# Where the state-space mixer's phase doublings and weight sums stand in the first gate-and-up stage

## The chip, the cores and the metric

The kernel runs on one core of one Trainium2 chip. The metric is the device time of one execution in microseconds (us). Three runs of the kernel before gave 2377.18, 2378.55 and 2381.32 us.

The engines are named as in the profile: PE is TensorE (matrix products, PEld its weight loads), DVE is VectorE, ACT is ScalarE, POOL is GpSimd, and SP is the engine whose queue issues all the DMA transfers spoken of here. Every engine works through its own instructions in a fixed order, and waits on semaphores for the others.

## The reference: what is computed

Two layers on a sequence of 1024 tokens of width 1024, in float32. Layer 0 mixes tokens by attention with a forget gate, layer 1 by a state-space mixer called S5. Behind each mixer comes a dense SwiGLU:

```
def swiglu(h, w_gate, w_up, w_down):
    return (jax.nn.silu(h @ w_gate) * (h @ w_up)) @ w_down
```

The S5 mixer needs, for 64 groups of 64 states, powers of a complex number `a` and a scaled input matrix:

```
    mag = jnp.exp(lam_re * dt)
    a_re = mag * jnp.cos(lam_im * dt)
    a_im = mag * jnp.sin(lam_im * dt)
...
    bb_re = z_re[..., None] * b_re - z_im[..., None] * b_im
    bb_im = z_re[..., None] * b_im + z_im[..., None] * b_re
```

None of these parameters depends on the tokens. So the kernel works them out long before layer 1 begins, beside the gate and up products of layer 0. The change lies there.

## The kernel before

**Gate and up.** `gate_up` runs once in each layer. It multiplies the normalized tokens by `w_gate` (called m = 0) and `w_up` (m = 1). It does so with a scheme that needs seven block products in place of eight, so sums and differences of the weight blocks are formed first. The 22 column blocks of each matrix are taken in 11 pairs, p = 0 to 10 (blocks p and p + 11). A pair has 14 steps on PE, two (m = 0, 1) for each of the seven products in `steps`; steps 0 and 1 are A11, 2 and 3 A12, 4 and 5 S1, 6 and 7 S2, 8 and 9 S3, 10 and 11 S4, 12 and 13 A22. A step is 4 blocks of k times 3 matmuls: each operand is split in a high part (`ah`, rounded by ACT, line 851) and a low part (`al`, the rest, by DVE, line 852), and three of the four products of parts are taken. All these matmuls are on line 882.

**Banks.** A step's result goes to a bank of PSUM: X for steps 0, 1, 6 to 9, 12 and 13, Y for steps 2 and 3, Z for steps 4, 5, 10 and 11, one bank for each m. X has two sets that alternate between pairs. Each step is evicted before its bank can be written again: steps 0 and 1 by an ACT copy (line 932), 2 and 3 by a DVE addition (line 934), 4 to 7 by ACT copies (lines 937 and 939), 8 and 9 by DVE (line 941), 10 and 11 by DVE (line 944). ACT applies silu on line 920.

**Weights of the next pair.** `load` fetches raw weight pages, on SP, as pages come free. `sa` forms the sums S1 and S2 (lines 864 and 865), `sb` S3 and S4 (lines 870 and 871) in the raw page itself. `prep` says behind which step each is written down; the scheduler may queue them sooner.

**The mixer's parameters.** `s5_params`, with `s5_small` in it, is a generator. It is carried on by a bit at the steps listed in the table `first`, which stands in `trunk` (pairs 0, 1 and 2; 5 and 12 in the others). Among its pieces are:
- the powers of `a` (`powers`, with `cmul`, lines 1211 to 1216);
- the phases `ph` of 15 multiples of an angle, by doubling: n = 1, 2, 4, 8, six DVE operations each (lines 1184 to 1189), on tiles of 64, 128, 256 and 448 elements a partition;
- `bb`, a `cmul` of 128x512 with the raw `b` (tile s5w0) and scratch (tile s5w1), and on ACT copies of it to `bs` (line 1272);
- the loads of `c_re` and `c_im` (line 1233) onto the pages of those two tiles, and their transposes on PE (line 1239), which ACT copies out to `cc` (line 1243);
- tables for 8 chunks of groups, built on POOL (lines 1269 to 1332).

The phases are read by `s5_rot`, which runs beside the down stage.

**What sets the order.** The framework plays the program through with its own estimates and queues, on each engine, what it holds ready first, by priority. Evictions are written under `high_priority`. Two calls bind it: `keep_in_program_order` queues an instruction behind all that was written down before it for its engine, and `issue_after` queues what is written inside it behind a named instruction on that one's engine. Both set a place in the queue and add no wait. Tiles are pages of rings: `R("bb")` and `R("s5t2")` are both page 28, s5w0 is page 34 and s5w1 page 32. A tile on a page waits until the last reader of the tile before it on that page is done. The doublings' scratch is a tile of the ring s5t2:

```
        kk = R("s5t2", (P, 2, 16, 32))
...
        self.bb = R("bb", (P, 2, 32, 16))
...
        craw = [R(f"s5w{i}", (P, 8, 2, HD)) for i in range(2)]
```

Of the kernel before, what the change touches and what calls it, by code (L numbers as in the profile page):

```python
# [12 lines left out]
ALU = mybir.AluOpType  # L13

P = 128
# [10 lines left out]
MAGIC = 1.5 * 2.0 ** 23  # L26
# [132 lines left out]
class Trunk:  # L159
# [668 lines left out]
    def gate_up(self, B, g_d, beside=iter(()), when=lambda p, s: False):  # L828
# [7 lines left out]
        nc, R = self.nc, self.R  # L836
        V = nc.vector
        n = NF // 2
        raws, S, E, Z, U = {}, {}, {}, {}, {}
# [5 lines left out]
        def split(ring, names, key, src):  # L845
            if ring == "a2":
                t = R("a2", (P, 2, 4, P), F32R)
                h, l = t[:, 0], t[:, 1]
            else:
                h, l = R(ring + "h", (P, 8, P), F32R), R(ring + "l", (P, 8, P), F32R)  # L850
            nc.scalar.copy(h, src)  # L851
            V.tensor_sub(l, src, f32(h))  # L852
            for i, x in enumerate(names):
                s = slice(4 * i, 4 * i + 4)
                E[key + (x,)] = h[:, s], l[:, s]
# [5 lines left out]
        def sa(p, m):  # L861
            r1, r2 = raws[p, m]
            t = S[p, m] = R("S", (P, 8, P))
            V.tensor_add(t[:, 0:4], r2[:, 0:4], r2[:, 4:8])
            V.tensor_sub(t[:, 4:8], t[:, 0:4], r1[:, 0:4])
            split("a", ("S1", "S2"), (p, m), t)

# [6 lines left out]
        def e4(p, m):  # L874
            split("a2", ("A22",), (p, m), raws.pop((p, m))[1][:, 4:8])

        def mm(p, m, a, b, bank, start):
            h, l = E.pop((p, m, a))
            for k in range(4):
                bh, bl = B(b, k)  # L880
                for i, (x, y) in enumerate(((h, bh), (h, bl), (l, bh))):
                    nc.tensor.matmul(bank, x[:, k], y, start=start and k == i == 0, stop=True, skip_group_check=True)  # L882

        lo, hi = slice(0, 512), slice(512, 1024)
# [18 lines left out]
        for p, s in order:  # L903
            if (p, s) == (2, 0):
                for r in ("s", "up"):
                    if len(R.r[r][0]) == 3:
                        R.set(**{r: R.r[r][0][::-1]})
            bank = {(x, m): self.bank(i + m, 1, (P, 512)) for x, i in (("X", (p % 2 * 2) ^ self.X0), ("Y", 4), ("Z", 6)) for m in (0, 1)}
            if s == 0:
                zs[p] = [[R(r)] for r in ("s", "ez" if p == 1 and "ez" in R.r else "up")]  # L910
                if p == 1:
                    R.r.pop("ez", None)
            if s == 4:
                for m, r in enumerate(("s", "up")):
                    zs[p][m].append(R(r))
            z = zs[p]

            def silu(m, x, src=None):
                if not m:
                    nc.scalar.activation(x, x if src is None else src, AF.Silu)  # L920

            def times(i, c, by=None):
                s, u = z[0][i][:, c], z[1][i][:, c]
                V.tensor_mul(s, s, u if by is None else by)  # L924

            m = s % 2
            a, b, x = steps[s // 2]
            mm(p, m, a, b, bank[x, m], s < 6)
            X, Y, Q = (bank[i, m] for i in "XYZ")
            with self.tc.high_priority(AHEAD):  # L930
                if s // 2 == 0:
                    nc.scalar.copy(z[m][0][:, lo], X)
                elif s // 2 == 1:
                    V.tensor_add(z[m][0][:, lo], z[m][0][:, lo], Y)
                    silu(m, z[m][0][:, lo])
                elif s // 2 == 2:
                    nc.scalar.copy(z[m][1][:, hi], Q)
                elif s // 2 == 3:
                    nc.scalar.copy(z[m][1][:, lo], X)  # L939
                elif s // 2 == 4:  # L940
                    V.tensor_add(z[m][1][:, hi], z[m][1][:, hi], X)
                    silu(m, z[m][1][:, hi])
                elif s // 2 == 5:
                    V.tensor_add(z[m][0][:, hi], z[m][1][:, lo], Q)
                    silu(m, z[m][0][:, hi])
                elif s == 12:
                    silu(m, z[m][1][:, lo], X)
                elif s == 13:
                    times(1, lo, X)
            if s == 3:  # L950
                times(0, lo)
            elif s == 9:
                times(1, hi)
            elif s == 11:
                times(0, hi)
                g0, g1, q0, q1 = *z[0], *z[1]
                V.tensor_add(q0[:, hi], g0[:, hi], g1[:, hi])
                V.tensor_sub(q0[:, lo], g0[:, lo], g0[:, hi])
                nc.sync.dma_start(g_d[0][p][:, lo], g0[:, lo])
                nc.sync.dma_start(g_d[1][p][:, hi], g1[:, hi])  # L960
                nc.sync.dma_start(g_d[2][p], q0)
            elif s == 13:
                V.tensor_sub(q1[:, lo], q0[:, hi], g0[:, lo])
                V.tensor_sub(q1[:, hi], g1[:, lo], q1[:, lo])
                nc.sync.dma_start(g_d[0][p][:, hi], g1[:, lo])
                nc.sync.dma_start(g_d[1][p][:, lo], q1[:, lo])
                nc.sync.dma_start(g_d[3][p], q1[:, hi])
            if (p, s) == (n - 1, 9):
                for i in range(self.taken, self.taken + 4):
                    self._load(i)  # L970
            if (p, s) == (1, 1):
                end()
            if (p, s) in ((1, 2), (1, 3), (0, 4)):
                B.late(f"T{s}")
            if p == 1 and s < 4:
                continue
            if s in prep and (p + 1 < n or s < 7):
                prep[s](p)
            elif s == 7:
                e4(p, 1)  # L980
            if p == 0 and s > 11:
                prep[s - 10](1)
            if when(p, s):
                next(beside, None)
        yield

    def down(self, finish, begin=lambda tb, m: None, beside=iter(()), steps=((),) * 3, extra=0, last=3,
# [89 lines left out]
    def s5_small(self):  # L1077


        nc, A, c, R = self.nc, self.A, self.cst, self.R  # L1080
        V = nc.vector
        tt, ts, stt = V.tensor_tensor, V.tensor_scalar, V.scalar_tensor_tensor
# [17 lines left out]
        ps = self.pb((0, 1), (P, 4, 32))  # L1100
# [26 lines left out]
        ang, n, r = (w[:, 8 + 3 * i:11 + 3 * i] for i in range(3))  # L1127
# [4 lines left out]
        C1 = 6.28125  # L1132
        C2 = math.floor((2 * math.pi - C1) * 2 ** 20) / 2 ** 20
        C3 = 2 * math.pi - C1 - C2
        LIM = 3.141592
# [24 lines left out]
        X = self.ph.rearrange("p i a n -> p n (i a)")  # L1160
# [5 lines left out]
        kk = R("s5t2", (P, 2, 16, 32))  # L1166

        def powers(X, top):
            n = 1
            while n < top:  # L1170
# [3 lines left out]
                          kk[:, 0, :c_], kk[:, 1, :c_])  # L1174
                n += c_

        yield
        powers(pw, 8)
        yield
        n, N = 1, kk.rearrange("p i n a -> p (i n a)").rearrange("p (n m) -> p n m", m=64)  # L1180
        while n < 15:
            c_ = min(n, 15 - n)
            x, q = X[:, n + 1:n + 1 + c_], N[:, :c_]
            tt(x, X[:, 1:1 + c_], X[:, n:n + 1].to_broadcast([P, c_, 64]), op=ALU.add)
            ts(q, x, 1.0 / (2 * math.pi), MAGIC, op0=ALU.mult, op1=ALU.add)
            V.tensor_scalar_sub(q, q, MAGIC)
            stt(x, q, -C1, x, op0=ALU.mult, op1=ALU.add)
            stt(x, q, C1 - 2 * math.pi, x, op0=ALU.mult, op1=ALU.add)
            ts(x, x, LIM, -LIM, op0=ALU.min, op1=ALU.max)
            n += c_  # L1190
            if n == 8:
                yield

        z = self.z = c.tile([P, 2, 32], F32, name="z5")
        u1, u2, u3, nre = tmp(), tmp(), tmp(), tmp()
        ar, ai = Pre[:, 1], Pim[:, 1]
# [21 lines left out]
    def s5_params(self):  # L1218


        nc, A, R = self.nc, self.A, self.R
# [3 lines left out]
        braw, kk = self.braw, R("s5w1", (P, 2, 32, 16))  # L1225
# [4 lines left out]
        craw = [R(f"s5w{i}", (P, 8, 2, HD)) for i in range(2)]  # L1230
# [4 lines left out]
        for i in range(2):  # L1235
            yield
            ps = self.S("psC", (P, 8, P))
            for t in range(8):
                nc.tensor.transpose(ps[:, t], craw[i][:, t].rearrange("p d s -> p (d s)"), self.ident)

            for d in range(2):
                r = slice(d * 64, d * 64 + 64)
                nc.scalar.copy(self.cc[r, i].rearrange("p (t a) c -> p t a c", t=8),
                               ps[r].rearrange("p t (a b c) -> p t a b c", b=2, c=16)[:, :, :, d])
# [353 lines left out]
def trunk(ctx: ExitStack, tc: tile.TileContext, A, out):  # L1598
    T = Trunk(ctx, tc, A, out)
    nc, R = T.nc, T.R  # L1600
# [87 lines left out]
    T.fox(hT, og_d, first_norm(range(2, 8), (2, 3, -2, -1)), OUT0)  # L1688
    xr = x0.rearrange("(p b) d -> p b d", b=8)
    R.set(hold=[28, 30, 31, 34, 36, 37], t1=[20], ah=[3, 4, 20], al=[5, 6, 21], er=[29, 32])  # L1690
    first = {0: (8, 10, 12), 1: (5, 6, 8, 10, 12), 2: (5, 8, 12)}
    B = Operands(T)
    gu = T.gate_up(B, g_d[0], T.s5_params(), lambda p, s: s in first.get(p, (5, 12)))
    end = T.out_proj(lambda tb: xr[:, tb, :], A["mix_post_gain"][0], A["ffn_pre_gain"][0], x1_d, turns, B, lambda: next(gu))
# [130 lines left out]
```

## Time and profile before

| | |
|---|---|
| median of 3 runs | 2378.55 us |
| profiled execution, its own time | 2381.82 us |
| its span | 2380.0 us |
| PE busy | 2343.3 us (98%) |
| DVE busy | 1676.1 us (70%) |
| ACT busy | 1197.9 us (50%) |
| POOL busy | 423.1 us (18%) |
| DMA | 320.61 MB, mean 135 GB/s |

The profile is of one execution, on one core. Times in it count from the start of the span. A row of a view in order of time has the start, the duration, the engine, the line, the operation and the tiles (output, arrow, inputs), and in brackets how long the engine was idle before it and what ended that. Matmuls are pipelined: a row's duration is longer than the distance to the next start. A row of the waits has who waited for whom, the total in us, the number of times, and the longest. In layer 0 the steps of gate and up begin at 735 us and end at about 1183; pair 2 lies from 813 to 861.

### The profile page before, as it was taken

What the parts mean: (1) busy time and instruction counts of PE and PEld (TensorE: products, weight loads), DVE (VectorE), ACT (ScalarE), POOL (GpSimd) and SP (SyncE); (2) the same over time, 40 slices, a digit from 0 to 9 for tenths busy, and PEclk for the clock granted to TensorE, in tenths of its full rate; (3) what the DMA queues carried; (4) which work ended last, traced back from release to release, by engine and by line L of the source; (5) the groups of instructions that cost most, each with busy time, mean ns of one, the idle gap of its engine ahead of it and who ended that gap; (6) DMA issues with size and microseconds to landing.
All of it is one profiled execution on the core that took longest, in us unless ns stands there. A gap on an engine that the chain in (4) does not pass through costs nothing.

```text
span 2380.0 us, 31540 instructions
## 1 busy us (share of the span) xinstructions
PE 2343.3 (98%) x11736; PEld 1945.8 (82%) x11736; DVE 1676.1 (70%) x2676; ACT 1197.9 (50%) x2032; POOL 423.1 (18%) x411
## 2 busy tenths in 40 slices
PE   8999999999999999999999999999999999999998
PEld 7788888888788778888888889988888888888887
DVE  6867777678778966666778686753795656555867
ACT  6766676677745334444554662332463333333443
POOL 3222221222200034545520002410000000000000
PEclk9999999999999999999999999999999999999999
DMA  5121112211433444343598752453434323237874
GB/s 162 36 63 53 55 50 65 64 45 58 139 128 111 120 116 139 118 138 118 179 331 310 269 178 93 125 161 107 131 102 142 111 93 107 93 120 257 287 247 168
DMA packets 256684, 320.61 MB, mean 135 GB/s; under 512 B 34313, under 2 KB 184129, under 8 KB 256530
## 3 DMA queue, kind: packets, MB, share of 16 engines
q1 hardware_dynamic: 256530, 318.59, 41.2%
q8 instruction: 92, 1.51, 0.3%
q14 instruction: 62, 0.51, 0.1%
HBM read 240.82 MB, written 77.72 MB: 134 GB/s over the span
## 4 chain that ended last, share of the span: by engine, by line
PE 80%; DVE 10%; ACT 5%; issue 3%; DMA 1%; POOL 1%; DVEq 0%; SPq 0%; ACTq 0%; POOLq 0%
PE ps L882 31%; PE ps L1003 16%; PE ps L274 7%; PE ps L275 7%; PE ps L276 7%; PE ps L644 2%; PE ps L625 2%; PE ps L586 1%; DVE ps L590 1%; PE ps L587 1%; DVE ptl L629 1%; DVE y L329 1%; ACT y L298 1%; POOL o L652 1%; DMA raw<-in_ffn_w_gate_dram 1%
## 5 line engine op out<-in xcount | busy, mean ns | idle before, releaser
L882 PE MATMUL ps<-B,ah 128*128 128x512 f32 x992 | 306.3, 390 | 0.8 <-DVE B L90 0.6
L1003 PE MATMUL ps<-wdh,gh 128*128 128x512 f32 x616 | 240.0, 390 | 0.6 <-DVE s L924 0.6
L1003 PE MATMUL ps<-wdl,gh 128*128 128x512 f32 x616 | 239.8, 389 | 0.0
L1003 PE MATMUL ps<-wdh,gl 128*128 128x512 f32 x616 | 239.6, 389 | 0.1
L882 PE MATMUL ps<-ops,ah 128*128 128x512 f32 x704 | 219.7, 393 | 2.0 <-ACT s L939 1.7
L882 PEld LDWEIGHTS ps<-B,ah 128*128 128x128 f32 x992 | 186.1, 188 | 40.7 <-DVE B L90 1.2
L274 PE MATMUL ps<-hT,wh 128*128 128x512 f32 x496 | 197.3, 398 | 0.7 <-DVE pt L465 0.2
L276 PE MATMUL ps<-hT,wl 128*128 128x512 f32 x496 | 194.9, 393 | 0.0
L275 PE MATMUL ps<-hT,wh 128*128 128x512 f32 x496 | 194.4, 392 | 0.0
L882 PE MATMUL ps<-B,al 128*128 128x512 f32 x496 | 193.0, 389 | 0.0
L255 ACT CAST gh<-gr 128x1024 fp32r<-128x1024 f32 (+1 forms) x78 | 81.1, 1040 | 161.4 <-PE ps L1003 132.4
L882 PEld LDWEIGHTS ps<-ops,ah 128*128 128x128 f32 x704 | 132.3, 189 | 31.6 <-ACT s L939 2.1
L256 DVE TENSOR_TENSOR gl<-gr,gh 128x1024 fp32r<-128x1024 f32 (+1 forms) x78 | 98.6, 1265 | 79.1 <-ACT gh L255 79.0
L852 DVE TENSOR_TENSOR al<-raw,ah 128x1024 fp32r<-128x1024 f32 x84 | 107.8, 1284 | 55.0 <-ACT ah L851 54.9
L629 DVE TENSOR_TENSOR ptl<-ps,pth 128x512 fp32r<-128x512 f32 x192 | 102.6, 551 | 55.2 <-ACT pth L628 54.4
L1761 POOL TENSOR_TENSOR y<-m,s 128x512 f32<-128x512 f32 x4 | 6.5, 1645 | 750.6 <-DVE m L1030 652.9
L882 PE MATMUL ps<-ops,al 128*128 128x512 f32 x352 | 137.7, 391 | 0.0
L581 POOL TENSOR_TENSOR An<-An,cmask 128x128 f32<-128x128 f32 x128 | 75.3, 590 | 344.5 <-DVE mx L590 317.3
L1003 PEld LDWEIGHTS ps<-wdh,gh 128*128 128x128 f32 x616 | 115.6, 188 | 25.2 <-DVE s L924 1.3
L1003 PEld LDWEIGHTS ps<-wdh,gl 128*128 128x128 f32 x616 | 115.6, 188 | 24.7 <-DVE gl L256 0.5
L1003 PEld LDWEIGHTS ps<-wdl,gh 128*128 128x128 f32 x616 | 115.6, 188 | 23.7
L851 ACT CAST ah<-raw 128x1024 fp32r<-128x1024 f32 x84 | 88.4, 1052 | 91.4 <-PE ps L882 83.1
(393 smaller groups left out, 5891.0 us busy)
## 6 DMA issues: line engine op xcount, KB each, us to landing
raw<-in_ffn_w_down_dram SPq DMA_DIRECT2D x98, 512.0 KB, 5.4
gr<-g_d SPq DMA_DIRECT2D x76, 512.0 KB, 4.8
raw<-in_ffn_w_gate_dram SPq DMA_DIRECT2D x44, 512.0 KB, 4.1
raw<-in_ffn_w_up_dram SPq DMA_DIRECT2D x44, 512.0 KB, 4.4
g_d<-s SPq DMA_DIRECT2D x66, 256.0 KB, 2.1
raw<-in_fox_w_in_dram SPq DMA_DIRECT2D x32, 512.0 KB, 4.3
g_d<-up SPq DMA_DIRECT2D x44, 256.0 KB, 2.9
g_d<-up SPq DMA_DIRECT2D x21, 512.0 KB, 2.7
```

What stands on the lines that cost most here:

```text
L255: self.hop = self.hcopy(h, src)
L256: self.lop = self.lsub.tensor_sub(l, src, f32(h))
L274: mm(ps, lh, rh, start=start, stop=False)
L275: mm(ps, lh, rl, start=False, stop=False)
L276: mm(ps, ll, rh, start=False, stop=stop)
L581: nc.gpsimd.tensor_add(An[h][:, qs], An[h][:, qs], self.cmask)
L625: nc.tensor.transpose(p2[:, i], p[:, (g + i) * P:(g + i + 1) * P], self.ident)
L629: nc.vector.tensor_sub(dl, p2[:, 0:n], f32(dh))
L851: nc.scalar.copy(h, src)
L852: V.tensor_sub(l, src, f32(h))
L882: nc.tensor.matmul(bank, x[:, k], y, start=start and k == i == 0, stop=True, skip_group_check=True)
L1003: nc.tensor.matmul(bank, x[:, j, t], y[:, j], start=start and i == 0, stop=True, skip_group_check=True)
```

## The change

Three edits:

1. The phase doublings leave `s5_small` and become a generator of their own, `phases`. It is carried on once in each pair from 4 on, at step 8. Pair 4 takes n = 1 and 2, pairs 5 and 6 the halves of n = 4, pairs 7 and 8 the halves of n = 8. The first operation of each half is pinned with `keep_in_program_order`. The scratch is now a part of the tile R2, and not the page that `bb` will use. The generator of the parameters has one halt less, and `first` one entry less in pair 1.
2. In `gate_up`, the first operation of `sa` is queued behind the last eviction of step 3 written down so far (`E[1]`). This holds for both layers.
3. The first of each group of eight transposes of c is pinned.

```
@@ gate_up: sa
-            V.tensor_add(t[:, 0:4], r2[:, 0:4], r2[:, 4:8])
+            with self.tc.issue_after(E[1].ins) if 1 in E else nullcontext():
+                V.tensor_add(t[:, 0:4], r2[:, 0:4], r2[:, 4:8])
@@ gate_up: the eviction of steps 2 and 3
-                    V.tensor_add(z[m][0][:, lo], z[m][0][:, lo], Y)
+                    E[m] = V.tensor_add(z[m][0][:, lo], z[m][0][:, lo], Y)
@@ gate_up: the end of a step
             if when(p, s):
                 next(beside, None)
+            if s == 8 and p > 3:
+                next(self.phases, None)
@@ s5_small
+        pin = self.tc.keep_in_program_order
+
+        def phases():
+            N = R2[:, 0:448].rearrange("p (n m) -> p n m", m=64)
+            for n in (1, 2, 4, 8):
+                c_ = min(n, 15 - n)
+                x, q = X[:, n + 1:n + 1 + c_], N[:, :c_]
+                pin(tt(x, X[:, 1:1 + c_], X[:, n:n + 1].to_broadcast([P, c_, 64]), op=ALU.add))
+                ts(q, x, 1.0 / (2 * math.pi), MAGIC, op0=ALU.mult, op1=ALU.add)
+                V.tensor_scalar_sub(q, q, MAGIC)
+                if n > 2:
+                    yield
+                pin(stt(x, q, -C1, x, op0=ALU.mult, op1=ALU.add))
+                stt(x, q, C1 - 2 * math.pi, x, op0=ALU.mult, op1=ALU.add)
+                ts(x, x, LIM, -LIM, op0=ALU.min, op1=ALU.max)
+                if n > 1:
+                    yield
+
+        self.phases = phases()
         yield
         powers(pw, 8)
         yield
-        n, N = 1, kk.rearrange("p i n a -> p (i n a)").rearrange("p (n m) -> p n m", m=64)
-        while n < 15:
...
-            n += c_
-            if n == 8:
-                yield
@@ s5_params: the transposes of c
-                nc.tensor.transpose(ps[:, t], craw[i][:, t].rearrange("p d s -> p (d s)"), self.ident)
+                op = nc.tensor.transpose(ps[:, t], craw[i][:, t].rearrange("p d s -> p (d s)"), self.ident)
+                if not t:
+                    self.tc.keep_in_program_order(op)
@@ trunk
-    first = {0: (8, 10, 12), 1: (5, 6, 8, 10, 12), 2: (5, 8, 12)}
+    first = {0: (8, 10, 12), 1: (5, 6, 8, 10), 2: (5, 8, 12)}
```

The orders below are of the built programs. Lines of the changed kernel are a little higher: 865 is 864 of before, 935 is 934, 942 is 941, 852 stays 852, 1187 to 1194 are the doublings, 1219 to 1224 are `cmul`, 1247 the transposes.

DVE, end of pair 1 and start of pair 2. R and s5t are the doublings' tiles, `s` and `up` those of the evictions, S the sums, al the low parts. Before:

```order
L1184 TENSOR_TENSOR R_775_7458<-R_775_7458 128x7x64
L864 TENSOR_TENSOR S_7921<-raw_7778 128x512
L1185 TENSOR_SCALAR s5t_777_7470<-R_775_7458 128x448
L934 TENSOR_TENSOR s_7689<-s_7689,ps 128x512
L1186 TENSOR_SCALAR s5t_777_7470<-s5t_777_7470 128x448
L852 TENSOR_TENSOR al_7735<-S_7731,ah_7734 128x1024
L1187 SCALAR_TENSOR_TENSOR R_775_7458<-s5t_777_7470,R_775_7458 128x7x64
L934 TENSOR_TENSOR up_7690<-up_7690,ps 128x512
L1188 SCALAR_TENSOR_TENSOR R_775_7458<-s5t_777_7470,R_775_7458 128x7x64
L924 TENSOR_TENSOR s_7689<-s_7689,up_7690 128x512
L1189 TENSOR_SCALAR R_775_7458<-R_775_7458 128x7x64
L1213 TENSOR_TENSOR bb_7657<-s5w_790_7655 128x512
```

And now the rows of the `bb` product, which begin behind an al and end ahead of the last product of pair 1 (L925):

```order
L852 TENSOR_TENSOR al_7589<-raw_7524,ah_7588 128x1024
L1219 TENSOR_TENSOR s5w_787_7592<-s5w_774_7455,z_7546 128x512
L945 TENSOR_TENSOR ez_7056<-up_7406,ps 128x512
L1220 TENSOR_TENSOR s5w_787_7592<-s5w_774_7455,z_7546 128x512
L925 TENSOR_TENSOR s_7055<-s_7055,ez_7056 128x512
L1221 TENSOR_TENSOR bb_7594<-s5w_787_7592 128x512
L958 TENSOR_TENSOR ez_7056<-s_7055,s_7405 128x512
L1222 TENSOR_TENSOR s5w_787_7592<-s5w_774_7455,z_7546 128x512
L1223 TENSOR_TENSOR s5w_787_7592<-s5w_774_7455,z_7546 128x512
L959 TENSOR_TENSOR ez_7056<-s_7055 128x512
L1224 TENSOR_TENSOR bb_7594<-s5w_787_7592 128x512
L925 TENSOR_TENSOR s_7405<-s_7405,ps 128x512
```

The product of `bb`, which stood behind the last doubling (L1189) in pair 2, now stands in pair 1, and between it and the eviction of step 2 (L935) there is no doubling. On SP the four c loads moved with it, from between two weight loads of pair 2 to just behind a store of pair 1; on ACT the four copies to `bs` moved ahead of pair 2's first eviction copy.

PE, pair 2. T and ops are tiles of the tokens, ah and al of the weights. Before, around the first group of transposes:

```order
L882 MATMUL ps<-ops_7114,al_7735 128x512
L882 MATMUL ps<-ops_7141,ah_7754 128x512
L1239 MATMUL ps<-ident,s5w_792_7664 128x128 x8
L882 MATMUL ps<-ops_7143,ah_7754 128x512
L882 MATMUL ps<-ops_7141,al_7755 128x512
```

Now:

```order
L883 MATMUL ps<-T_6113,ah_7710 128x512 x2
L883 MATMUL ps<-T_6113,al_7711 128x512
L1247 MATMUL ps<-ident,s5w_789_7601 128x128 x8
L883 MATMUL ps<-ops_7113,ah_7630 128x512
L883 MATMUL ps<-ops_7115,ah_7630 128x512
```

The group stood behind the first matmul of step 8 and now stands between steps 5 and 6. The second group stays behind step 8; nothing else moves on PE or on POOL.

DVE, start of pair 5. L864 (now 865) are sums of pair 6, L934 (now 935) the evictions of steps 2 and 3. Before:

```order
L964 TENSOR_TENSOR up_8348<-s_8347,up_8348 128x512
L864 TENSOR_TENSOR S_8811<-raw_8666 128x512
L934 TENSOR_TENSOR s_8577<-s_8577,ps 128x512
L852 TENSOR_TENSOR al_8623<-S_8619,ah_8622 128x1024
L864 TENSOR_TENSOR S_8918<-raw_8740 128x512
L934 TENSOR_TENSOR up_8578<-up_8578,ps 128x512
```

The same place in the changed kernel:

```order
L965 TENSOR_TENSOR up_8324<-s_8323,up_8324 128x512
L935 TENSOR_TENSOR s_8565<-s_8565,ps 128x512
L852 TENSOR_TENSOR al_8611<-S_8607,ah_8610 128x1024
L935 TENSOR_TENSOR up_8566<-up_8566,ps 128x512
L865 TENSOR_TENSOR S_8802<-raw_8654 128x512
L925 TENSOR_TENSOR s_8565<-s_8565,up_8566 128x512
L852 TENSOR_TENSOR al_8631<-raw_8341,ah_8630 128x1024
L865 TENSOR_TENSOR S_8909<-raw_8728 128x512
```

Both sums moved behind the second eviction. The same move is found in pairs 3 to 9 of this stage and in the second gate and up.

More of the change, by code (lines that the diff above doesn't have):

```diff
@@ L1179, in s5_small @@
         yield
-        n, N = 1, kk.rearrange("p i n a -> p (i n a)").rearrange("p (n m) -> p n m", m=64)
-        while n < 15:
[L1182 to L1189, printed above, removed]
-            n += c_
-            if n == 8:
-                yield
         z = self.z = c.tile([P, 2, 32], F32, name="z5")
```

## The prediction

> **What bounds the kernel now.** I read the page first, then a table by stage of the busy time, then the waits of TensorE (PE) in the first gate and up stage, and last that stage in order of time, engine by engine. From the page, the busy time of each engine and the chain of waits that ended last:
>
> ```profile
> PE 2343.3 (98%) x11736; PEld 1945.8 (82%) x11736; DVE 1676.1 (70%) x2676; ACT 1197.9 (50%) x2032; POOL 423.1 (18%) x411
> PE 80%; DVE 10%; ACT 5%; issue 3%; DMA 1%; POOL 1%; DVEq 0%; SPq 0%; ACTq 0%; POOLq 0%
> ```
>
> TensorE is busy for all but 36.7 us of the span of 2380.0 (2380.0 - 2343.3), so a saving can only be idle TensorE time, or time at a lower clock. The stage that the diff touches shows both in one place. By stretches of 10 us (stretch, sum, then busy time of PE, PEld, DVE, ACT, POOL, granted clock, DMA share, GB/s):
>
> ```profile
> 824.00:834.00 10.00, 8.37 (x38) 6.59 (x37) 9.93 (x15) 2.88 (x6) 0.00 (x0) 1.00 0.26 80
> 834.00:844.00 10.00, 6.77 (x27) 5.34 (x26) 6.93 (x10) 4.75 (x9) 0.00 (x0) 0.77 1.02 209
> 844.00:854.00 10.00, 10.00 (x45) 8.21 (x44) 3.81 (x5) 2.60 (x4) 5.34 (x5) 0.89 0.05 19
> ```
>
> The waits of TensorE over the whole first gate and up stage (730 to 1182 us) are three, one occurrence each:
>
> ```profile
> PE ps L882 <- ACT s L939: 1.7, 1, 1.7
> PE ps L882 <- DVE al L852: 1.6, 1, 1.6
> PE ps L1239 <- DMA s5w<-in_s_c_re_dram: 1.5, 1, 1.5
> ```
>
> In order of time they lie in pair 2 (start, duration; the bracket is the idle time before the row and what ended it):
>
> ```profile
> 829.10 0.50 PE L882 MATMUL ps<-T,al 128*128 128x512 f32 x1 [1.63 <-DVE al L852]
> 838.81 0.50 PE L882 MATMUL ps<-ops,ah 128*128 128x512 f32 x1 [1.72 <-ACT s L939]
> 840.83 1.94 PE L1239 MATMUL ps<-ident,s5w 128*128 128x128 f32 x8 [1.51 <-DMA s5w<-in_s_c_re_dram]
> ...
> 843.42 1.05 PE L882 MATMUL ps<-ops,ah 128*128 128x512 f32 x2
> ...
> 844.70 1.05 PE L882 MATMUL ps<-ops,ah 128*128 128x512 f32 x2
> ...
> 846.80 1.04 PE L1239 MATMUL ps<-ident,s5w 128*128 128x128 f32 x8
> 847.60 0.72 PE L882 MATMUL ps<-ops,ah 128*128 128x512 f32 x2
> ...
> 861.34 0.62 PE L882 MATMUL ps<-B,ah 128*128 128x512 f32 x2
> ...
> 862.02 0.62 PE L882 MATMUL ps<-B,ah 128*128 128x512 f32 x2
> ```
>
> The rows at 861.34 and 862.02 give the full pace, 0.68 us for three matmuls. Those at 843.42 and 844.70 give 1.28: behind the second and third wait TensorE runs at about half pace until some 846. Behind the first wait alone the clock of its stretch stayed 1.00.
>
> **What pair 2 can give.** The ScalarE (ACT) copy of a pair's first product marks each pair:
>
> ```profile
> 816.17 0.59 ACT L932 COPY s<-ps 128x512 f32<-128x512 f32 x1 [2.10 <-PE ps L882]
> ...
> 864.26 0.59 ACT L932 COPY s<-ps 128x512 f32<-128x512 f32 x1 [2.10 <-PE ps L882]
> ...
> 904.44 0.59 ACT L932 COPY s<-ps 128x512 f32<-128x512 f32 x1 [2.10 <-DMA g_d<-s]
> ```
>
> Pair 2 took 48.09 us, pair 3 40.18. A pair has 14 steps of 12 matmuls, 56 threes: 56 x 0.68 = 38.08. Pair 2 also holds two groups of eight transposes, 0.80 each (846.80 to 847.60): 38.08 + 1.60 = 39.68. So 48.09 - 39.68 = 8.41 us are lost: 1.63 + 1.72 + 1.51 = 4.86 waiting, and 3.55 by the clock and by restarts. That is the ceiling here, 0.35% of the time.
>
> **First part: the doublings leave VectorE (DVE), and what was behind them.** The end of the backlog on DVE, and ScalarE and the SP queue behind it:
>
> ```profile
> 809.07 1.22 DVE L852 TENSOR_TENSOR al<-raw,ah 128x1024 fp32r<-128x1024 f32 x1
> ...
> 827.52 0.39 DVE L1186 TENSOR_SCALAR s5t<-s5t 128x448 f32<-128x448 f32 x1
> 827.82 1.22 DVE L852 TENSOR_TENSOR al<-S,ah 128x1024 fp32r<-128x1024 f32 x1
> ...
> 830.42 0.99 DVE L1188 SCALAR_TENSOR_TENSOR R<-s5t,R 128x448 f32<-128x448 f32 x1
> ...
> 831.89 0.66 DVE L1189 TENSOR_SCALAR R<-R 128x448 f32<-128x448 f32 x1
> 832.41 0.71 DVE L1213 TENSOR_TENSOR bb<-s5w 128x512 f32<-128x512 f32 x1
> ...
> 834.75 0.72 DVE L1215 TENSOR_TENSOR s5w<-s5w,z 128x512 f32<-128x512 f32 x1
> ...
> 835.96 0.72 DVE L1216 TENSOR_TENSOR bb<-s5w 128x512 f32<-128x512 f32 x1
> ```
> ```profile
> 836.71 0.50 ACT L1272 COPY R<-bb 64x64 f32<-64x64 f32 x2 [2.57 <-DVE bb L1216]
> ...
> 838.18 0.58 ACT L939 COPY s<-ps 128x512 f32<-128x512 f32 x1
> ```
> ```profile
> 835.50 1.03 SPq L1233 DMA_DIRECT2D s5w<-in_s_c_re_dram  x2
> ```
>
> All three waits have one root. bb lies on the memory page that the doublings used as scratch (ring s5t2 and ring bb are both page 28), so its product (L1211 to L1216) could end only behind L1189 at 831.89. The three follow:
> - Wait 1: the low half of pair 2's second sums (al, 827.82 to 829.04) stood behind doublings and was late for step 5.
> - Wait 2: ScalarE stood in its in-order queue at the copy of bb until L1216 ended at 836.68, so the copy that frees the bank of step 6 (L939) came at 838.18.
> - Wait 3: the load of c_re goes onto the page of b's raw data, so it left at 835.50, behind L1215's end at 835.47, and its transposes waited.
>
> In the new order ten operations of 128x512 follow the al that ends at 810.29, down to the last of the bb product. Two of them start 1.21 apart over two (834.75 and 835.96), 0.605 each, so bb is complete by 810.29 + 6.05 = 816.3, 20 us earlier. On from there: one product out of PSUM (0.6), one al (1.2), seven operations of 128x512 (4.2) and the eviction of step 2 (0.6; step 2 itself ends two steps behind the copy at 816.17, at 821.6) end at 822.9, and the al that step 5 needs at 824.1. TensorE asks for it at 829.10 - 1.63 = 827.5: 3.4 us to spare, wait 1 goes. ScalarE's bb copies end at about 816.9, ahead of the eviction copy that was at 816.17; that costs 0.7 on a bank that is written again only in step 6, ten us later: wait 2 goes, nothing paid. The c_re load leaves behind the eighth of the ten operations, at 815.1. Before, it was issued at 835.50 and its transposes began at 840.83, 5.3 us later; so both halves are there by 820.5. The transposes now stand pinned behind step 5, which ends near 816.17 + 5 x 2.72 = 829.8 (a step is four threes, 2.72): 9 us to spare, wait 3 goes. All later matmuls stand behind these transposes, so each us beyond that would be a us of the path; and ScalarE's copies of them (L1243) stand ahead of the eviction of step 6, which ends 6 us behind them. The four c loads now stand on SP ahead of pair 1's last stores and the next two weight loads, and hold them until bb is there at 816.3. The first of those weight loads waits for its own page in any case, until the fourth of the seven operations, 820.5. I cost that at nothing; if the cover failed, a weight page of pair 3 would be late, and pair 3 begins only at 861.34 - 8.41 = 852.9. With no idle stretch left nothing lowers the clock: all 8.41 us go.
>
> By the Trainium skill, page "TensorE: Matmul & The Clock Gate", section "Part 1: The HAM clock gate", a gap must fill a window of about 3.4 us before the clock halves, and the row of the first, single gap (clock 1.00) agrees. By that rule the 3.55 us would go even if one of the last two waits stayed.
>
> **The doublings in pairs 4 to 8.** 24 operations: of 448 elements the rows above have 0.39 to 0.99 us, the smaller sizes less. In pair 4 twelve of 64 and 128 elements are put around the evictions of steps 8 and 9 (L941); in pairs 5 to 8 one or two stand in front of step 9's eviction, up to 1.0 us in all. What hides them is the distance from there to the bank's next use; in pair 4:
>
> ```profile
> 970.67 0.67 DVE L941 TENSOR_TENSOR s<-s,ps 128x512 f32<-128x512 f32 x1
> ```
> ```profile
> 978.53 0.60 ACT L920 ACTIVATE s<-ps 128x512 f32<-128x512 f32 x1 [1.90 <-PE ps L882]
> ```
>
> The bank freed at 971.34 is written again by step 12, which ends at 978.5 and so begins at 975.8: 4.5 us to spare, and the bank of step 9 has one step more less one eviction. Cost taken: 0; bounds 0, and 1.0 in each of five pairs.
>
> **The sums behind step 3's eviction.** Before, the first sum of the next pair stands at the head of DVE's queue and waits for its weights:
>
> ```profile
> 949.77 0.99 DVE L864 TENSOR_TENSOR S<-raw 128x512 f32<-128x512 f32 x1 [5.92 <-DMA raw<-in_ffn_w_gate_dram]
> 950.68 0.68 DVE L934 TENSOR_TENSOR s<-s,ps 128x512 f32<-128x512 f32 x1
> ```
>
> Steps 2 and 3 are evicted behind that wait. In the new order the evictions go first. But TensorE waits nowhere in pairs 3 to 10 (three waits in all, above), so this is worth 0 there; it lengthens nothing either, since these sums belong to the next pair. The same edit acts in the second gate and up, where TensorE has no wait of this kind. Bounds: 0.7 either way, one eviction (row 950.68).
>
> **The sum.** On the profiled execution: 2381.82 (span 2380.0 and 1.82 around it) - 8.41 = 2373.4. It lies 3.3 above the median of the three runs, 2378.55, and 0.5 above their highest (2377.18 to 2381.32). The waits follow from the order of instructions, so I take the same 8.4 off the median: **2370.1 us**.
>
> **Rivals.**
> - *A part of the loss stays.* One piece of the new chain is later than I worked out (the c_re transfer beside the stores of pair 1, or the al of step 5), and one wait of 1.5 to 1.7 is left, with or without its 3.55 of slow clock: 2370.1 + 1.6 = 2371.7, to 2370.1 + 5.2 = 2375.3. For it: the four loads move into a busy time of SP. Against: 3.4 and 9 us of slack.
> - *The gain is given back.* A later stage is limited by transfers, and the saved time is waited off there: 2377 to 2379. For it: DMA share is up to 1.02 in single stretches. Against: TensorE's share of the chain is 80%, and none of its waits behind this stage is for a load; the longest is for POOL:
>
> ```profile
> PE ps L1412 <- POOL S L1394: 2.3, 1, 2.3
> ```
>
> - *Slower: the doublings beside GpSimd (POOL).* In the old place POOL did nothing; in pairs 4 to 8 it builds tables. The same operation there:
>
> ```profile
> 821.79 0.71 DVE L871 TENSOR_TENSOR raw<-raw,S 128x512 f32<-128x512 f32 x1
> ...
> 857.53 1.77 DVE L871 TENSOR_TENSOR raw<-raw,S 128x512 f32<-128x512 f32 x1
> ```
> ```profile
> 857.13 3.32 POOL L1273 TENSOR_TENSOR s5w<-s5w 64x512 f32<-64x512 f32 x2
> ```
>
> 2.5 times as long. It decides once a doubling group pushes an eviction beyond the 4.5 us: at 2.5 times, one of 1.0 becomes 2.5, still inside. It would take a delay of 4.5 + 8.4/5 = 6.2 us in each of five pairs to cancel the gain; at 7.5 us in each the kernel takes 2370.1 + 5 x 3.0 = 2385. The Trainium skill, page "SBUF — State Buffer", section "SBUF: two separate sides", says that VectorE and GpSimd lock a shared port pair for a whole instruction and the other blocks. The rows at 857 agree, and the rule speaks against this place for the doublings.
>
> **Chances.** Forecast 0.78; a part stays 0.10; given back 0.08; slower 0.04. A measurement of this kernel can tell about 0.2%, 4.8 us, from no change, so faster means below 2373.8. The forecast lies there, and of the second case about 0.07: faster 0.85, same 0.03 + 0.08 = 0.11, slower 0.04. Range: downward the runs' spread below their median, 1.4, and 0.7 for the sums: 2368.0. Upward one wait left and the spread above the median, 1.6 + 2.8, and the 0.3 that rounding adds: 2374.8.
>
> **What would show it.** Right: pair 2 about 39.7 us long (first copy to first copy), no TensorE wait in the first gate and up stage, granted clock 1.00 in every stretch of it, bb's last operation near 816, c_re landed by 822, doublings in pairs 4 to 8 with no TensorE wait beside them. Wrong: a wait at the pinned transposes, a new wait at step 12 of pairs 4 to 8, or the same gate and up shortened but a later stage longer by as much.

## The result, and the profile after

The changed kernel takes 2386.46 us (median of 9 runs, 2383.47 to 2389.36) where the kernel before takes 2378.94 (9 runs, 2377.13 to 2381.32): a ratio of 1.0033, 95% interval 1.0022 to 1.0043. It is slower by some 7.5 us; 8.4 faster was forecast. The profiled run took 2386.42 us, its span 2384.6.

The forecast gain is there. The stretches of 10 us in pair 2 (stretch, sum, busy time of PE, PEld, DVE, ACT, POOL, granted clock, DMA share, GB/s), after:

```profile
824.00:834.00 10.00, 10.00 (x50) 8.37 (x49) 4.73 (x6) 4.03 (x7) 0.00 (x0) 1.00 0.58 156
834.00:844.00 10.00, 10.00 (x49) 8.35 (x49) 6.86 (x9) 3.44 (x6) 4.63 (x4) 1.00 0.19 52
844.00:854.00 10.00, 10.00 (x46) 8.27 (x45) 9.71 (x9) 4.17 (x6) 6.92 (x5) 1.00 0.07 26
```

TensorE no longer idles there, and the clock is 1.00 throughout. But further on in the stage there are new waits. All the waits of TensorE that the view lists for the first gate and up, in the changed kernel:

```profile
PE ps L1297 <- POOL s5w L1283: 9.9, 6, 2.3
```

L1297 are 16 small products that take a table which GpSimd builds for one chunk of groups (L1279 to L1283). There is one chunk in a pair. Where the waits lie is told by the first copy of each pair, from pair 2 on (the first row is the copy to `bs` ahead of it):

```profile
815.08 0.50 ACT L1282 COPY R<-bb 64x64 f32<-64x64 f32 x2 [1.86 <-DVE bb L1224]
815.60 0.59 ACT L933 COPY s<-ps 128x512 f32<-128x512 f32 x1
854.87 0.59 ACT L933 COPY s<-ps 128x512 f32<-128x512 f32 x1 [2.10 <-PE ps L883]
895.05 0.59 ACT L933 COPY s<-ps 128x512 f32<-128x512 f32 x1 [2.10 <-PE ps L883]
935.23 0.59 ACT L933 COPY s<-ps 128x512 f32<-128x512 f32 x1 [2.10 <-PE ps L883]
980.70 0.59 ACT L933 COPY s<-ps 128x512 f32<-128x512 f32 x1 [2.10 <-PE ps L883]
1020.88 0.59 ACT L933 COPY s<-ps 128x512 f32<-128x512 f32 x1 [2.09 <-PE ps L883]
1066.35 0.59 ACT L933 COPY s<-ps 128x512 f32<-128x512 f32 x1 [2.10 <-PE ps L883]
1106.53 0.59 ACT L933 COPY s<-ps 128x512 f32<-128x512 f32 x1 [2.10 <-PE ps L883]
1151.94 0.59 ACT L933 COPY s<-ps 128x512 f32<-128x512 f32 x1 [2.09 <-PE ps L883]
```

The differences are 40.18 for pairs 3, 4, 6 and 8 as before, and 45.47, 45.47 and 45.41 for pairs 5, 7 and 9. For pair 2 the copy is no good mark: it stood behind the copies to `bs` and came 3.52 us behind the pair's first matmul, where it is 2.92 before. So pair 2 is counted on TensorE, from its own first matmul to that of pair 3:

```profile
812.08 0.62 PE L883 MATMUL ps<-B,ah 128*128 128x512 f32 x2
...
851.95 0.62 PE L883 MATMUL ps<-B,ah 128*128 128x512 f32 x2
```

That is 39.87 us, against 48.09 before (813.25 to 861.34). So 8.22 us are won in pair 2 and 3 x 5.27 = 15.8 lost behind it: 7.6 net, where the medians are 7.5 apart. (The two profiled runs are only 4.6 apart: the run of the kernel before was 2.9 above its median, and it was slower in the stages around this one.)

Where the lost time begins is read backward from the wait in pair 5. TensorE, after:

```profile
951.11 0.39 PE L1297 MATMUL ps<-s5w,R 128*16 128x128 f32 x2 [2.32 <-POOL s5w L1283]
952.44 1.62 PE L1297 MATMUL ps<-s5w,R 128*16 128x128 f32 x14 [0.94 <-POOL s5w L1283]
```

GpSimd, the first and the last operation of the table:

```profile
939.65 1.11 POOL L1279 TENSOR_TENSOR s5w<-cc,pw 128x512 f32<-128x512 f32 x1 [18.16 <-DMA T_d<-s5w]
...
949.47 2.92 POOL L1283 TENSOR_TENSOR s5w<-s5w 64x512 f32<-64x512 f32 x2
```

GpSimd waited for the landing of the store of T, a tile of the chunk before, since it builds the next chunk's table on the page that this store reads. The queue of SP, on which the store is issued:

```profile
924.96 0.35 SPq L961 DMA_DIRECT2D g_d<-s  x1
933.71 0.34 SPq L962 DMA_DIRECT2D g_d<-up  x1
934.14 0.38 SPq L1268 DMA_DIRECT2D T_d<-s5w  x1
935.51 0.32 SPq L966 DMA_DIRECT2D g_d<-s  x1
```

T itself had been ready for 2.9 us: ScalarE's copy of it ends at 931.26.

```profile
930.24 1.02 ACT L1267 COPY s5w<-ps 128x1024 f32<-128x1024 f32 x1
```

So the store of T stood on SP behind the store of L962. That one takes `up` (q0 in the code), which VectorE finishes with L959:

```profile
921.10 0.67 DVE L942 TENSOR_TENSOR s<-s,ps 128x512 f32<-128x512 f32 x1
921.70 0.27 DVE L1187 TENSOR_TENSOR R<-R 128x64 f32<-128x64 f32 x1
...
926.68 0.28 DVE L1194 TENSOR_SCALAR R<-R 128x128 f32<-128x128 f32 x1
926.87 0.68 DVE L945 TENSOR_TENSOR s<-s,ps 128x512 f32<-128x512 f32 x1
...
932.99 0.69 DVE L959 TENSOR_TENSOR up<-s 128x512 f32<-128x512 f32 x1
```

Here are the twelve doublings of pair 4 (the first and the last are shown). From the first of them to L959 VectorE has no idle time. The same places in the kernel before, in pairs of the same numbers, in the order GpSimd, TensorE, SP, ScalarE:

```profile
944.16 1.11 POOL L1269 TENSOR_TENSOR s5w<-cc,pw 128x512 f32<-128x512 f32 x1 [12.07 <-DMA T_d<-s5w]
...
951.82 3.85 POOL L1273 TENSOR_TENSOR s5w<-s5w 64x512 f32<-64x512 f32 x2
```
```profile
958.11 1.05 PE L1287 MATMUL ps<-s5w,R 128*16 128x128 f32 x16
```
```profile
940.00 0.34 SPq L961 DMA_DIRECT2D g_d<-up  x1
940.68 0.32 SPq L1258 DMA_DIRECT2D T_d<-s5w  x1
```
```profile
939.64 1.01 ACT L1257 COPY s5w<-ps 128x1024 f32<-128x1024 f32 x1
```

Measured from pair 4's first copy (904.44 before, 895.05 after), T is ready at 36.21 in both. The store of q0 goes at 35.56 before and at 38.66 after (+3.10, for 3.4 us of doublings), the store of T at 36.24 and 39.09 (+2.85). It lands 3.48 us behind its issue before and 5.51 after (+2.03). GpSimd's table takes 11.5 before and 12.7 after (+1.2). Together 6.1 us later, on a slack of 2.44: before, the table ends at 955.67 and TensorE takes it at 958.11. The 3.7 us that are left over are the two waits, 2.32 and 0.94, and the matmuls between them. The rest of the 5.3 is pace: the clock of 950 to 1000 is 0.97. Two terms of the 6.1 are not explained by the queue alone: the longer landing (see the end), and the longer table. The table now lies beside more of VectorE's own work; its third and fourth operation take 3.91 us from 941.91 on, and 2.63 before (946.41).

### The profile page after: what moved, and what is told of

Read it like the earlier page. It is cut to its first block, busy times and chain, and to the rows that moved or that the text cites. A ratio compares the mean times of both kernels' runs of the same rounds, so it can differ in the third digit from the quotient of the medians.

```text
span 2384.6 us, 31551 instructions
## 1 busy us (share of the span) xinstructions
PE 2342.8 (98%) x11736; PEld 1944.0 (82%) x11736; DVE 1683.7 (71%) x2676; ACT 1197.2 (50%) x2032; POOL 427.1 (18%) x411
## 3 DMA queue, kind: packets, MB, share of 16 engines
q8 instruction: 92, 1.51, 0.3%
## 4 chain that ended last, share of the span: by engine, by line
PE 81%; DVE 9%; ACT 5%; issue 3%; POOL 2%; DMA 1%; DVEq 0%; SPq 0%; ACTq 0%; POOLq 0%
PE ps L883 32%; PE ps L1006 16%; PE ps L274 7%; PE ps L275 7%; PE ps L276 7%; PE ps L644 2%; PE ps L625 2%; PE ps L586 1%; PE ps L587 1%; DVE ps L590 1%; POOL s5w L1283 1%; DVE y L329 1%; ACT y L298 1%; DVE ptl L629 1%; DMA T_d<-s5w 1%
## 5 line engine op out<-in xcount | busy, mean ns | idle before, releaser
L1006 PE MATMUL ps<-wdh,gh 128*128 128x512 f32 x616 | 240.0, 390 | 0.6 <-DVE s L925 0.6
L1006 PE MATMUL ps<-wdl,gh 128*128 128x512 f32 x616 | 239.8, 389 | 0.0
L1006 PE MATMUL ps<-wdh,gl 128*128 128x512 f32 x616 | 239.6, 389 | 0.1
L256 DVE TENSOR_TENSOR gl<-gr,gh 128x1024 fp32r<-128x1024 f32 (+1 forms) x78 | 99.0, 1270 | 79.3 <-ACT gh L255 78.9
L852 DVE TENSOR_TENSOR al<-raw,ah 128x1024 fp32r<-128x1024 f32 x84 | 115.2, 1373 | 54.5 <-ACT ah L851 54.3
L1006 PEld LDWEIGHTS ps<-wdh,gh 128*128 128x128 f32 x616 | 115.6, 188 | 25.4 <-DVE s L925 1.3
L1006 PEld LDWEIGHTS ps<-wdh,gl 128*128 128x128 f32 x616 | 115.6, 188 | 24.3 <-DVE gl L256 0.5
L1006 PEld LDWEIGHTS ps<-wdl,gh 128*128 128x128 f32 x616 | 115.6, 188 | 23.8
```

The lines of the kernel that those rows point to most:

```text
L256: self.lop = self.lsub.tensor_sub(l, src, f32(h))
L1006: nc.tensor.matmul(bank, x[:, j, t], y[:, j], start=start and i == 0, stop=True, skip_group_check=True)
```

## The experiments

The theory, called queue: the doublings at step 8 make q0 late, the store of T stands behind q0's store on SP, and GpSimd's table comes late. Rivals: the doublings slow GpSimd by a port that the two engines share (port); the sums that were moved behind step 3's evictions cause it (sums). Against the port speaks already the trace of the changed kernel: GpSimd is idle from 921.49 to 939.65 (the row at 939.65, 18.16 of idle time), and the doublings of pair 4 lie from 921.70 to 926.96. In pairs 5 to 8 too they begin 0.2 us behind GpSimd's last operation and end long before its next. The kernel before took 2379.8 us (24 runs, 2376.36 to 2383.54) beside the first four kernels, and 2379.47 (22 runs, 2376.28 to 2382.57) beside the last three.

**1. No doublings at all.** The changed kernel without the 24 operations; the phases are set to zero by GpSimd early, so layer 1 turns by wrong phases.

```
+        nc.gpsimd.memset(X[:, 2:16], 0.0)
...
-            for n in (1, 2, 4, 8):
+            for n in ():
...
+            yield
```

> The changed kernel with the 24 doublings left out altogether (the phases are set to zero by GpSimd early, so layer 1 is computed with wrong phases); the other edits stay. Theory (queue): the doublings in pair 4 hold VectorE back, the store of q0 that waits for VectorE goes later on SP, the store of T behind it too, GpSimd waits for that store to have its page back, and TensorE waits for GpSimd's table in pairs 5, 7 and 9. Then all three waits go and the saving of pair 2 is left: 2378.9 - 8.3 = 2370.6, pairs 3 to 9 all 40.2 long. Rival (port): the doublings slow GpSimd by the shared port; the same 2370.6. Rival (sums): the moved sums cause the waits; then they stay: about 2385.

Measured: 2372.55 us (7 runs, 2371.14 to 2374.1), ratio 0.9971 (0.996 to 0.9983). All pairs from 3 on are 40.18 long, pair 2 39.87 (counted on TensorE, as above), the store of T goes 36.0 to 36.7 us behind a pair's first copy in the rows I took, and GpSimd's waits for it are 12 to 13.6. So the waits come of the doublings; the sums, which stayed where the change puts them, bring none by themselves. The time is 2 us above the 2370.6 expected (the kernel before was 0.9 higher beside these runs); the rest is not explained.

**2. The doublings at the end of step 13.** There q0's last operation has been queued.

```
-            if s == 8 and p > 3:
+            if s == 13 and p > 3:
```

> All doublings kept, but carried on at step 13 of pairs 4 to 8 and not at step 8: on VectorE they then stand behind the pair's last operation, where VectorE waits for TensorE in any case and nothing of SP's queue waits for them. Queue: no waits, 2370.6. Port: there they lie beside GpSimd's table building (it runs over the first 10 us of a pair), which is on the path, so the waits stay or grow: 2386 or more. Sums: 2386, as the change.

Measured: 2373.66 us (10 runs, 2371.05 to 2375.51), ratio 0.9973 (0.9964 to 0.9982). TensorE's waits in this stage and at the start of down (L1006), with one left in the stage, which is another:

```profile
PE ps L883 <- DVE al L852: 1.0, 1, 1.0
PE ps L1006 <- DVE s L925: 0.6, 1, 0.6
```

SP at the end of pair 4:

```profile
931.52 0.34 SPq L962 DMA_DIRECT2D g_d<-up  x1
931.95 0.38 SPq L1268 DMA_DIRECT2D T_d<-s5w  x1
```

T's store is at 36.35 behind the first copy again (895.60). The median is 3 us above the forecast 2370.6; the wait that is left makes pair 5 1.3 us longer. Here doublings and table lie side by side, so this also speaks on the port. GpSimd's table behind pair 4, first and last operation, and VectorE:

```profile
935.70 1.10 POOL L1279 TENSOR_TENSOR s5w<-cc,pw 128x512 f32<-128x512 f32 x1 [13.21 <-DMA T_d<-s5w]
...
943.04 2.68 POOL L1283 TENSOR_TENSOR s5w<-s5w 64x512 f32<-64x512 f32 x2
```
```profile
935.49 0.19 DVE L1189 TENSOR_SCALAR R<-R 128x64 f32<-128x64 f32 x1
...
936.97 1.07 DVE L1193 SCALAR_TENSOR_TENSOR R<-R,R 128x64 f32<-128x64 f32 x1
938.07 1.29 DVE L1194 TENSOR_SCALAR R<-R 128x64 f32<-128x64 f32 x1
```

The table takes 10.0 us, and 11.1 in experiment 1, which has no doublings: beside these small operations GpSimd isn't slowed. VectorE is: operations of 64 elements go from 0.2 us to between 1.1 and 1.3 as soon as GpSimd runs. That delays the al of step 5 and gives the wait of 0.98 that is left. Beside the larger doublings of pairs 5 to 8 GpSimd is slowed as well: the table takes 11.4 to 12.9 us there, against 11.1 to 11.2 in experiment 1, most behind pair 8 (448 elements), where its first two operations take 1.57 and 1.87 in place of 1.11:

```profile
1097.29 1.57 POOL L1279 TENSOR_TENSOR s5w<-cc,pw 128x512 f32<-128x512 f32 x1 [13.25 <-DMA T_d<-s5w]
1098.83 1.87 POOL L1280 TENSOR_TENSOR s5w<-cc,pw 128x512 f32<-128x512 f32 x1
```

These 1.8 us are less than the slack of 2.44 worked out above for pair 5, and TensorE doesn't wait. So the port costs both engines where doublings and table meet; in the change they don't meet, and it is not what the change lost its time to.

**3. The store of T on ScalarE's queue.** The doublings stay at step 8.

```
-            nc.sync.dma_start(self.T_d[ch], T)
+            nc.scalar.dma_start(self.T_d[ch], T)
```

> The changed kernel, doublings in their place at step 8, with one edit: the store of T is issued by ScalarE, which has just written T, and not by SP, where it stands behind the store of q0. Queue: T is stored without waiting for VectorE, GpSimd starts on time, the waits of pairs 5, 7 and 9 go: 2370.6 to 2372. Port and sums: the waits stay, about 2386.

Measured: 2375.38 us (10 runs, 2372.26 to 2376.91), ratio 0.9981 (0.9971 to 0.999). The end of pair 4, on ScalarE, SP and GpSimd:

```profile
929.97 1.02 ACT L1267 COPY s5w<-ps 128x1024 f32<-128x1024 f32 x1
931.02 0.33 ACTq L1268 DMA_DIRECT2D T_d<-s5w  x1
```
```profile
933.62 0.34 SPq L962 DMA_DIRECT2D g_d<-up  x1
```
```profile
933.76 1.41 POOL L1279 TENSOR_TENSOR s5w<-cc,pw 128x512 f32<-128x512 f32 x1 [12.36 <-DMA T_d<-s5w]
```

q0's store is as late as in the changed kernel (38.66 behind the first copy at 894.96), but T's goes at once, lands 2.74 us later, and all pairs from 3 on are 40.18 again. This takes the link itself away, with the doublings as they were (the scheduler also changed the order of other stores on SP): the queue theory holds. The median is 3.4 us above the range expected, and the gain some 2 us short of experiment 2's; a wait of 1.5 that the others don't have stands at the start of the down stage (for `gl`, L256), whose order the scheduler changed.

**4. The sums back in their old place.** Doublings at step 8.

```
-            with self.tc.issue_after(E[1].ins) if 1 in E else nullcontext():
-                V.tensor_add(t[:, 0:4], r2[:, 0:4], r2[:, 4:8])
+            V.tensor_add(t[:, 0:4], r2[:, 0:4], r2[:, 4:8])
```

> The changed kernel with edit 2 undone: the next pair's sums are not held behind step 3's eviction. Queue and port: the waits stay, about 2386. Sums: the waits go, 2370.6.

Measured: 2385.86 us (6 runs, 2382.5 to 2392.7), ratio 1.0027 (1.0013 to 1.0041). The waits for GpSimd stay:

```profile
PE ps L1296 <- POOL s5w L1282: 4.8, 4, 1.8
PE ps L882 <- DVE al L852: 2.0, 1, 2.0
```

The sums are not the cause. The waits for GpSimd lie in pairs 5, 7 and 8 (there only 0.2), and the one of 2.0 for an al in pair 9; whether edit 2 is worth something here these runs can't tell.

**5. The kernel before, with its scratch alone on another page.** The doublings stay where they were.

```
-        n, N = 1, kk.rearrange("p i n a -> p (i n a)").rearrange("p (n m) -> p n m", m=64)
+        n, N = 1, R2[:, 0:448].rearrange("p (n m) -> p n m", m=64)
```

> The kernel before, with the doublings left where they were; only their scratch goes from the page that bb will use to R2. Theory of one root (the shared page made bb late, and all three old waits came of it): the waits for s, al and the c load in pair 2 go or shrink to under 1 us together, pair 2 is 39 to 41 us long, pairs 3 to 10 stay 40.18, no wait for GpSimd, some 2371 to 2373 (before: 2379 to 2380). Rival, the length of the backlog (24 doublings on VectorE cost their time wherever their scratch lies): the wait for al stays at 1.6, pair 2 is 41.5 to 45, 2373 to 2377. Rival, nothing of it lay in the scratch: three waits, 48 us, 2379.

Measured: 2375.33 us (11 runs, 2373.82 to 2377.9), ratio 0.9982 (0.9973 to 0.9991). TensorE's waits in the stage and at the start of down (L1003):

```profile
PE ps L882 <- DVE al L852: 1.0, 2, 0.5
PE ps L1003 <- DVE s L924: 0.6, 1, 0.6
PE ps L882 <- ACT ah L851: 0.2, 1, 0.2
```

The waits for `s` and for c are gone, the one for al has shrunk from 1.63 to 0.52. So the shared page was the root of the two, and of most of the third, as the prediction read it. The backlog keeps a price of its own: 0.76 us of waits in pair 2 and 0.53 in pair 3. The first matmuls of pairs 2 and 3 are these:

```profile
811.76 0.62 PE L882 MATMUL ps<-B,ah 128*128 128x512 f32 x2
...
853.03 0.62 PE L882 MATMUL ps<-B,ah 128*128 128x512 f32 x2
```

So pair 2 is 41.27 long, a little above the range of the root theory and below that of the backlog rival, and 1.40 more than in the changed kernel; pair 3, up to 894.03, is 41.00, 0.82 more than elsewhere. These 2.2 us are what the doublings still cost in their old place, and about what the time lies above the root theory's range.

**6. The doublings of pair 4 alone at step 8.** Those of pairs 5 to 8 are left out, and their phases are zero, so layer 1 turns by wrong phases.

```
+        nc.gpsimd.memset(X[:, 2:16], 0.0)
...
-            for n in (1, 2, 4, 8):
+            for n in (1, 2):
```

> The changed kernel with only the twelve doublings of pair 4 (n = 1 and 2) at step 8; those of pairs 5 to 8 are left out and their phases are zero, so layer 1 turns by wrong phases. Queue theory, each stall from the doublings of its own pair: table store of pair 4 some 39 us behind the pair's first copy, one stall of TensorE for GpSimd in pair 5 (45.5 us), pairs 6 to 10 at 40.18, the store there at 36.1; 2372.5 + 5.3 = 2377.8. Rival, a delay once begun comes back by itself every second pair: stalls in pairs 7 and 9 too, 2386. Rival, twelve small operations are not enough and the stalls are of the large ones: no stall, 2372.5.

Measured: 2378.41 us (10 runs, 2376.37 to 2381.97), ratio 0.9995 (0.9986 to 1.0004). TensorE's waits for GpSimd in the stage:

```profile
PE ps L1298 <- POOL s5w L1284: 3.4, 2, 2.3
```

One stall, in pair 5 (46.64 us); pairs 6 to 10 are 40.18. T's store in pair 4 goes 39.5 behind the first copy. So a delay once begun doesn't come back by itself: the stalls in pairs 7 and 9 of the changed kernel need the doublings that come after pair 4's. Which of them is not separated. In pair 6 of the changed kernel the store of T goes 39.32 behind the first copy, 3.3 later than before, while that pair's own doublings take only 1.7 us. VectorE was late there already ahead of them: the eviction of step 8 starts 27.94 behind the first copy, and 26.41 in pair 6 of this run. So the doublings of pair 5 bear on the stall in pair 7 too, as far as these two traces tell.

**7. Step 13, and the twelve of pair 4 divided over pairs 3 and 4.**

```
-            if s == 8 and p > 3:
+            if s == 13 and p > 2:
...
-                if n > 1:
-                    yield
+                yield
```

> All doublings done, at the end of step 13 in place of step 8, and the twelve of pair 4 divided over pairs 3 and 4. Queue theory: no wait for GpSimd, and the one wait of 0.98 us that was left at the start of pair 5 with all twelve there goes: all pairs from 3 on at 40.18 but for at most 0.5 in one; some 1 us under the version with twelve, 2372 to 2373 where before is 2379.5. Rival, six small operations still make al late: a wait of about 0.5 to 1 in pairs 4 and 5 each, 2374.

Measured: 2372.42 us (6 runs, 2370.88 to 2373.26), ratio 0.9968 (0.9956 to 0.998). TensorE waits nowhere in the stage; the first wait is at the start of down:

```profile
PE ps L1006 <- DVE s L925: 1.7, 1, 1.7
```

All pairs from 3 on are 40.18, pair 2 39.86. This is the lowest median of the versions that do all the work, 7.1 us below the kernel before, and it is as low as the version without the doublings: here they cost nothing that can be measured.

## Why the prediction was wrong

- **What bounds the kernel, and the gain in pair 2: right.** Forecast 39.7 us and 8.41 won, measured 39.87 and 8.22 on TensorE. Between first copies, the mark that the prediction names, it is 39.27: the copies to `bs` hold pair 2's first copy by 0.6 us, and the prediction had put that at 0.7, with nothing paid for it. The low part that step 5 needs was finished at 822.74 (forecast 824.1), the last operation of `bb` at 815.05 (816.3), and the transposes at 828.41 waited for nothing. That the waits for `s` and for c, and most of the one for al, had one root is shown by experiment 5.
- **The pinned transposes, 0 beyond the gain.** Without the pin, on the version of experiment 2, the order on every engine is the same row for row, so this was not run by itself: the new place of the transposes comes of `bb` being ready, not of the pin.
- **The sums behind step 3's eviction, 0: no loss by experiment 1**, which keeps them and has no wait for it. Whether they win anything was not run without the doublings.
- **"The doublings in pairs 4 to 8": this step failed.** It took their cost as 0 with bounds of 0 and 1.0 in each of five pairs, and "what hides them is the distance from there to the bank's next use". It asked only the evictions that stand behind the doublings for their deadline, and those did hold: no wait for a bank came. (The two rows it gives for pair 4, at 970.67 and 978.53, are of pair 5 of the kernel before; those of pair 4, at 930.00 and 938.63, leave 5.2 by the same sum in place of 4.5.) It didn't follow the rest of VectorE's queue. Behind the evictions stand L958 and L959, behind them a store on SP, behind that store another one on the same queue that belongs to other work, behind that GpSimd's table, and behind that TensorE. Measured: 5.3 us in each of three pairs, not 0 and not 1.0. The slack of that chain was 2.44 us, and all its links were in the trace of before: T ready at 940.65, q0's store at 940.00, T's at 940.68, GpSimd's start at 944.16 on that landing, its end at 955.67, TensorE at 958.11.
- **The rival on the slower side** named GpSimd and the doublings, but by the port, and put the point of decision at an eviction (6.2 us in each of five pairs). Its premise, that GpSimd builds tables where the doublings stand, didn't hold: the trace of the changed kernel has GpSimd idle beside all of them. And by experiment 3 the loss goes, with the doublings untouched, when one store changes its queue. The Trainium skill, page "SBUF — State Buffer", section "SBUF: two separate sides", has the loser of the shared port blocked for a whole instruction; the rows of experiment 2 agree, VectorE's beside the small doublings (from 0.2 us to between 1.1 and 1.3) and GpSimd's beside the large ones (from 1.11 to 1.57 and 1.87).
- **The clock.** The rule cited, of the Trainium skill, page "TensorE: Matmul & The Clock Gate", section "Part 1: The HAM clock gate", was that a gap must fill a window of about 3.4 us. The waits of 2.32 and 0.94 with two small matmuls between them lowered the granted clock to 0.97 over 50 us; the single wait of 0.98 in experiment 2 left it at 1.00. Two short gaps that lie close together, within 3.65 us, were enough here. The prediction's own row of the kernel before had shown it (1.72 and 1.51, clock 0.77).
- **The chances.** 0.85 for faster took the waits for the only uncertainty, and 0.04 for slower was the price of a mechanism that I had looked for at one place only.

## What to carry to other kernels

When work is put onto an engine that is busy without a gap, every instruction behind it is late by its length until the next idle time: follow each of these to its readers, through the DMA queues, where a store waits behind another store's data, up to the engine that sets the end, and take the smallest slack on the way. The DMA issues of one engine go in order, and so tie together work that has no data in common (T's store stood ready for 2.9 us behind that of q0). Before moving work off a busy place, see whether a shared page alone is the cause: another scratch tile by itself gave 4.1 us here (experiment 5), of the 7.1 of the best version. And before a mark on one engine is taken for the length of a stage, see that the mark itself didn't move: the first copy of pair 2 did, by 0.6 us here and by more in experiment 5.

## What the runs showed that I had not expected

- The same store of 512 KB landed 2.74 us behind its issue alone at the queue's head (experiment 3), 3.48 in the kernel before, and 5.51 when it went 2.85 us later, with the next stores issued 1.37 us behind it. Why 2.85 us of delay cost 2 more was not tried; that the transfers overlap more is only a reading.
- A VectorE operation of 64 elements a partition takes 0.19 to 0.28 us with GpSimd idle, and 1.07 to 1.29 beside it (experiment 2): in proportion small operations pay the most, some five times.
- The three stalls lie in every second pair, which looks like a rhythm of its own. Experiment 6 shows that one stall alone doesn't bring the next; why the doublings of pairs 5 and 7 bring none in pairs 6 and 8 was not run by itself.
